# A two-layer decoder on one core: the mixers' turned tiles move from SyncE's queue to GpSimd's, and some turns go to TensorE

## The chip, the core and the metric

The kernel runs on one core of one Trainium2 chip. A core has a matrix engine (TensorE, PE in the profile; its weight loads are PEld), a vector engine (VectorE, DVE), a scalar engine (ScalarE, ACT), a general engine (GpSimd, POOL) and SyncE (SP), which here only issues transfers. Each engine works through its own instructions in order, and they wait for one another by semaphores. Data lies in SBUF (128 partitions), matmuls write to PSUM, and transfers (DMA) move data between SBUF and the device's memory. An engine that issues a transfer puts it in its own queue.

The metric is the time of the device in microseconds for one execution. The kernel before took 2466.73 us (median of 3 runs, 2465.54 to 2467.15).

## The reference

Two layers over 256 tokens of width 2048, batch 1. All inputs are float32.

```python
def hybrid_mixer(h, positions, w_in, sinks, lb, attn_gain, hgrn_gain, w_out):
    proj = h @ w_in                                   # 2048 -> 5632
    q, k, v, hq, hf, hi, hg = jnp.split(proj, SPLIT_POINTS, axis=-1)
    q = rope(q.reshape(B, S, N_Q_HEADS, HEAD_DIM), positions)
    k = rope(k.reshape(B, S, N_KV_HEADS, HEAD_DIM), positions)
...
    attn = rms_norm(sliding_window_attention(q, k, v, sinks), attn_gain)
    f = lbf + (1.0 - lbf) * jax.nn.sigmoid(z)         # z = hf
    log_f = jnp.log(f)
    k_in = (1.0 - lbf) * jax.nn.sigmoid(-z)
    hq_ = jax.nn.silu(hq.astype(jnp.float32))
    o = hgrn2_chunkwise(hq_.reshape(shp), k_in.reshape(shp), hi.reshape(...), log_f.reshape(shp))
    o = rms_norm(o, hgrn_gain.reshape(HGRN_HEADS, HGRN_VDIM)).reshape(B, S, HGRN_WIDTH)
    hgrn = (o * jax.nn.silu(hg.astype(jnp.float32))).astype(h.dtype)
    return jnp.concatenate([attn, hgrn], axis=-1) @ w_out

for i in range(DEPTH):                                # DEPTH = 2
    x = x + rms_norm(hybrid_mixer(rms_norm(x, pre_mix_gain[i]), ...), post_mix_gain[i])
    h = rms_norm(x, pre_ffn_gain[i])
    f = (jax.nn.silu(h @ w_ffn_gate[i]) * (h @ w_ffn_up[i])) @ w_ffn_down[i]
    x = x + rms_norm(f, post_ffn_gain[i])
    gate = jax.nn.sigmoid(rms_norm(x, ple_gain[i]) @ w_ple_gate[i])
    x = x + (p[i] @ w_ple_proj[i]) * gate
```

The attention has 16 query heads of 64 over 4 key heads, a window of 128 tokens and a sink for each head. The recurrence `hgrn2_chunkwise` has 8 heads of 128; its gate is f, its query hq, its value hi.

## The kernel before

**Strips.** Every projection is cut into strips of 512 output columns (`strip`, L249). A strip runs over eight chunks of 256 rows of the weight. `load_w` (L239) loads a chunk (512 KB, issued by SyncE, four buffers `wr`), and `split` (L172) makes a high part `wh` on ScalarE (L174) and a low part `wl` on VectorE (L175), eight buffers each. For each half t of the tokens and each 128 rows come three matmuls of 512 columns (L261, L262, L264) into an accumulator `acc` in PSUM; there are four such accumulators and each strip takes two. Without skew a strip has 96 matmuls. When an accumulator is complete, `done(t, ps)` reads it out.

**Ticks.** After each chunk `tick` (L94) counts one up, moves the running generators by one step, and calls what `later(n, fn)` has put off by n ticks. A tick without other work is 12 matmuls. This sets the order in which work is written down; the order on each engine then follows the times that the program's ordering step reckons with, so that independent instructions of one engine can change places.

**Turned tiles.** A matmul takes its left side with the contracted dimension on the partitions, so results have to be turned before they are used again. There are two ways in the kernel. `split_T` (L184) transposes 128x128 blocks on TensorE into a PSUM bank `ms` (four banks, also used by the attention and the recurrence) and splits from there. `shuffled` (L204) turns 32x32 blocks on VectorE (L208) into a buffer b, stores b to a tile `turn` in device memory (L211), and reads it back with four transfers (L214) into a buffer d, from which ScalarE and VectorE go on. All five transfers are issued by SyncE, between the loads of weights. b, d and most short-lived tiles come from the pool `nat`, which has nine buffers.

**The mixer**, in order of its strips: key and value (`done_kv`, L491), two strips of queries (`done_q(half)`, L501), then for each of two groups of four recurrence heads the gate f (`done_f`, L620), the query (`done_q`, L638), the value i (`done_i`, L780) and the output gate g (`done_g`, L803). Keys and queries are rotated with two products on VectorE (L482) and two additions on GpSimd (L489) before they are turned. `attend` (L512) waits five ticks after the turn, copies the tile (L516) and runs the scores (L541), the transposes of the probabilities (L577) and the values (L592) between the strips' matmuls. After the second half it turns the attention's output (L524), and splits it five ticks later. In the recurrence f is turned and read four ticks later (L628, L629), q 5 - t ticks later (L651); with q's second half the generator `levels` (L731) starts, which multiplies queries and keys level by level (L737, L700 with the copies L709, L765), and `out` (L786) makes the output, with a small power on GpSimd (L155). `done_g` multiplies it by the gate's silu (L806, L808), turns it and splits it four ticks later (L229, L230). Slot D is used in turn by `ao`, `qd`, `qf` and the value `hv`.

The output projection follows (four strips over the turned mixer outputs `mix`; chunks 6 and 7 read the last group's), then the feed-forward part, where `done_up` (L867) turns its tiles by `shuffled` except in one case by `split_T`, and the embedding gate, whose `turn` (L932) turns x for the next layer.

Of the kernel before, what the change touches and what calls it, by code (L numbers as in the profile page):

```python
# [11 lines left out]
AF = mybir.ActivationFunctionType  # L12
# [3 lines left out]
P = 128  # L16
# [30 lines left out]
def decoder(ctx: ExitStack, tc: tile.TileContext, x, p, positions, w_in, attn_sinks,  # L47
# [3 lines left out]
    nc = tc.nc  # L51
# [20 lines left out]
    def later(n, fn):  # L72

        queue.append((clock[0] + n, fn))

    marks = {}
# [126 lines left out]

    def shuffled(src, n=4):  # L204


        b = nat((P, n * P))
        V.transpose(b.rearrange("p (q k j) -> p k q j", q=4, k=n),  # L208
                    src.rearrange("p (k q j) -> p k q j", k=n, q=4))
        m = dp.tile([4, 32, 4, n * 32], F32, tag="turn", name="turn")  # L210
        nc.sync.dma_start(m.rearrange("a i q f -> (a i) (q f)"), b)  # L211
        d = nat((P, n * P))
        for q in range(4):
            nc.sync.dma_start(d[q * 32:(q + 1) * 32].rearrange("i (a f) -> i a f", a=4),  # L214
                              m[:, :, q].rearrange("a i f -> i a f"))
        return d.rearrange("p (a k j) -> p k a j", a=4, k=n)

    def quarters(a):

        return a.rearrange("p k (a j) -> p k a j", a=4)  # L220

    def split_shuffled(d, gcols, hl, t):
        h, lo = (quarters(a[:, :, t * P:(t + 1) * P]) for a in hl)
        if gcols is None:
            split(d, h, lo)
            return
        for b in range(4):
            g = gcols[:, b:b + 1]
            marks["x"] = S.activation(h[:, b], d[:, b], AF.Copy, scale=g)  # L229
            V.scalar_tensor_tensor(lo[:, b], d[:, b], g, h[:, b].bitcast(F32),  # L230
                                   op0=ALU.mult, op1=ALU.subtract)
# [17 lines left out]
    def strip(lhs, w, col, done, nch=8, row0=0, skew=0, psum=None, pre=None):  # L249
# [4 lines left out]
        def part(t, c, lows=(0, 1)):  # L254
            hi, lo = ws[c]
            for k in range(2):
# [6 lines left out]
                if 1 in lows:  # L263
                    marks[t, c] = T.matmul(ps[t], xh, lo[:, k], start=False, stop=last)  # L264

# [189 lines left out]
    for l in range(DEPTH):  # L455
# [35 lines left out]
        def done_kv(t, ps):  # L491
# [6 lines left out]
            d = shuffled(o[:, 0:256], 2)  # L498
            later(8 - t, lambda: S.copy(quarters(kT[:, :, t * P:(t + 1) * P]), d))

# [11 lines left out]
        def attend(half, t, o):  # L512
            d = shuffled(o)
            for _ in range(5):
                yield
            S.copy(quarters(qT[half][:, :, t * P:(t + 1) * P]), d)  # L516
            yield
# [90 lines left out]
        class Rec:  # L608
# [11 lines left out]
            def done_f(s, t, ps):  # L620
                z = nat()
                S.activation(z, ps, AF.Copy, scale=rx(t)[:, 0:1])

                d = shuffled(z)

                def turn():
                    cols = slice(t * P, (t + 1) * P)
                    S.activation(quarters(s.f[:, :, cols]), d, AF.Sigmoid)  # L628
                    S.activation(quarters(s.k[:, :, cols]), d, AF.Sigmoid, scale=-1.0)  # L629
                    for h in range(4):  # L630
# [4 lines left out]
                                        None, op0=ALU.mult)  # L635
                later(4, turn)

            def done_q(s, t, ps):  # L638
# [6 lines left out]

                d = shuffled(sg)

                def turn():
                    raw = s.qd[:, :, t, 0:P]
                    cols = slice(t * P, (t + 1) * P)  # L650
                    S.copy(quarters(raw), d)  # L651

# [5 lines left out]
                    if t == 1:  # L658
                        start(s.levels())
                later(5 - t, turn)  # L660

# [141 lines left out]
            def done_g(s, t, ps):  # L803
# [6 lines left out]
                if c not in mix:  # L810
                    mix[c] = new_ck()
                d = shuffled(o)
                later(4, lambda: split_shuffled(d, gain_cols(112, l, 8)[:, 4 * s.grp:4 * s.grp + 4],
                                                mix[c], t))

# [38 lines left out]
        for gi, glen in enumerate(FF_GROUPS):  # L854
            hid = []
            for j in range(glen):
# [10 lines left out]
                def done_up(t, ps, hl=hl, gate=gate, j=j):  # L867
                    V.scalar_tensor_tensor(gate[t], ps, rx2(t)[:, 0:1], gate[t],  # L868
                                           op0=ALU.mult, op1=ALU.mult)
                    if glen == 2 and j == 1:  # L870
                        later(2, lambda g=gate[t], hl=hl: split_T(blocks4(g), None, hl, t))
                        return
                    d = shuffled(gate[t])
                    later(3, lambda: split_shuffled(d, None, hl, t))
# [98 lines left out]
```

## Time and profile before

| | |
|---|---|
| median of 3 runs | 2466.73 us (2465.54 to 2467.15) |
| the profiled execution | 2461.75 us |
| its span, from the first instruction to the last | 2460.0 us |
| matmuls on TensorE (PE) | 11245 |
| VectorE, ScalarE, GpSimd busy | 61%, 48%, 4% |
| transfers of turned tiles | 90 stores, 360 reads |
| one store of 256 KB, from issue to landing (median) | 2.5 us |
| one read of 64 KB (median) | 3.7 us |

The profile is of one execution. Its times are in microseconds from the start of the span. Rows name the line of the kernel, the engine, the operation, the tile written and the tiles read. The waits say who waited for whom; the releaser named is the one that came last. Durations of matmuls are those of a pipeline: each lasts 0.39 us in the records while the next starts 0.23 us after it, so start times tell the pace.

### The profile page before, as it was taken

How to read it: one execution, taken by the hardware profiler on the slowest of the kernel's cores; microseconds unless marked ns; L12 is line 12 of the kernel's file. 1: busy time of each engine (PE TensorE's matmuls, PEld its weight loads, DVE VectorE, ACT ScalarE, POOL GpSimd, SP SyncE). 2: the span in 40 equal slices, each digit the busy share in tenths (PEclk: the TensorE clock that was granted, in tenths of full speed). 3: DMA queues.
4: the chain of work that ended last, by engine and by line, in shares of the span. 5: the costliest groups of instructions: out<-in, count | busy, mean ns of one | idle time of the engine just before them, and what ended most of it. 6: DMA issues, size and time to landing. Idle time of an engine off the chain costs nothing.

```text
span 2460.0 us, 30961 instructions
## 1 busy us (share of the span) xinstructions
PE 2431.3 (99%) x11245; PEld 2005.3 (82%) x11245; DVE 1491.9 (61%) x1991; ACT 1187.0 (48%) x1684; POOL 98.5 (4%) x213
## 2 busy tenths in 40 slices
PE   9999999999999999999999999999999999999999
PEld 7887887888888888887888878878888888888877
DVE  7678866545555554557667688565455555555674
ACT  6564446444434434446556454464444444444463
POOL 3100001000000000001001000010000000000010
PEclk9999999999999999999999999999999999999999
DMA  8665665767667766764775756656677676677753
GB/s 265 200 194 172 203 192 163 231 190 213 208 211 209 211 211 195 226 218 155 249 224 165 218 181 196 204 176 219 189 211 224 198 209 214 207 211 212 221 169 130
DMA packets 299065, 497.60 MB, mean 202 GB/s; under 512 B 23424, under 2 KB 68896, under 8 KB 298912
## 3 DMA queue, kind: packets, MB, share of 16 engines
q1 hardware_dynamic: 298608, 495.54, 65.9%
q8 instruction: 88, 1.44, 0.2%
q14 instruction: 65, 0.53, 0.1%
q10 hardware_dynamic: 240, 0.07, 0.0%
q0 software_dynamic: 64, 0.02, 0.0%
HBM read 470.38 MB, written 25.17 MB: 201 GB/s over the span
## 4 chain that ended last, share of the span: by engine, by line
PE 91%; DVE 3%; DMA 2%; ACT 2%; issue 1%; POOL 0%; SPq 0%; ACTq 0%; DVEq 0%; POOLq 0%
PE acc L261 29%; PE acc L262 29%; PE acc L264 29%; DMA wr<-in_w_in_dram 1%; DVE wl L175 1%; PE ms L592 1%; DMA nat<-turn 1%; PE ms L700 1%; DMA turn<-nat 1%; ACT wh L174 1%; PE ms L189 0%; ACT junk L170 0%; PE ms L737 0%; PE ms L765 0%; ACT nat L560 0%
## 5 line engine op out<-in xcount | busy, mean ns | idle before, releaser
L175 DVE TENSOR_TENSOR wl<-wr,wh 128x1024 fp32r<-128x1024 f32 x840 | 1025.4, 1224 | 828.8 <-ACT wh L174 821.4
L174 ACT CAST wh<-wr 128x1024 fp32r<-128x1024 f32 x840 | 882.9, 1053 | 1085.0 <-PE acc L262 955.0
L261 PE MATMUL acc<-wh,ck 128*128 128x512 f32 x3328 | 1302.3, 392 | 14.6 <-ACT ck L200 4.6
L262 PE MATMUL acc<-wh,ck 128*128 128x512 f32 x3328 | 1300.0, 391 | 1.3 <-DVE ck L201 1.2
L264 PE MATMUL acc<-wl,ck 128*128 128x512 f32 x3328 | 1298.1, 390 | 0.0
L261 PEld LDWEIGHTS acc<-wh,ck 128*128 128x128 f32 x3328 | 625.8, 188 | 152.4 <-ACT ck L200 8.9
L262 PEld LDWEIGHTS acc<-wh,ck 128*128 128x128 f32 x3328 | 625.8, 188 | 134.0 <-DVE ck L201 4.8
L264 PEld LDWEIGHTS acc<-wl,ck 128*128 128x128 f32 x3328 | 625.9, 188 | 128.9
L200 ACT ACTIVATE ck<-ms,gT 128x128 fp32r<-128x128 f32 x160 | 50.3, 370 | 15.0 <-DVE ck L201 7.2
L160 POOL TENSOR_TENSOR tiny<-ssf 128x1 f32<-128x1 f32 x4 | 2.1, 536 | 1361.5 <-ACT junk L170 1361.2
L201 DVE SCALAR_TENSOR_TENSOR ck<-ms,gT,ck 128x128 fp32r<-128x128 f32 x160 | 48.5, 347 | 13.4 <-ACT ck L200 12.9
L208 DVE STREAM_TRANSPOSE nat<-nat 128x512 f32<-128x512 f32 (+1 forms) x68 | 46.9, 690 | 10.5 <-POOL nat L489 9.4
L892 DVE TENSOR_TENSOR macc<-acc,macc 128x512 f32<-128x512 f32 x48 | 33.0, 688 | 5.0 <-PE acc L264 4.5
L862 ACT ACTIVATE nat<-acc,ry 128x512 f32<-128x512 f32 x44 | 30.2, 687 | 10.7 <-PE acc L264 10.7
L229 ACT ACTIVATE ck<-nat,gT 128x128 fp32r<-128x128 f32 x88 | 28.1, 391 | 13.3 <-DMA nat<-turn 13.2
L170 ACT ACTIVATE junk<-x 128x512 f32<-128x512 f32 x48 | 30.3, 631 | 8.6 <-DVE x L925 4.4
L868 DVE SCALAR_TENSOR_TENSOR nat<-acc,ry,nat 128x512 f32<-128x512 f32 x44 | 32.4, 748 | 0.1
L230 DVE SCALAR_TENSOR_TENSOR ck<-nat,gT,ck 128x128 fp32r<-128x128 f32 x88 | 25.5, 348 | 9.5 <-ACT ck L229 9.5
L175 DVE TENSOR_TENSOR ck<-nat,ck 128x512 fp32r<-128x512 f32 x42 | 28.9, 687 | 0.1
L174 ACT CAST ck<-nat 128x512 fp32r<-128x512 f32 x42 | 26.0, 618 | 3.8 <-DVE nat L181 3.8
L560 ACT ACTIVATE nat<-nat,tiny 128x128 f32<-128x128 f32 x64 | 24.8, 389 | 4.3 <-DVE tiny L557 4.2
L592 PEld LDWEIGHTS ms<-vv,nat 128*128 128x128 f32 x192 | 23.2, 191 | 3.6 <-ACT nat L580 2.7
(192 smaller groups left out, 886.5 us busy)
## 6 DMA issues: line engine op xcount, KB each, us to landing
wr<-in_w_in_dram SPq DMA_DIRECT2D x176, 512.0 KB, 4.5
wr<-in_w_ffn_gate_dram SPq DMA_DIRECT2D x176, 512.0 KB, 3.9
wr<-in_w_ffn_up_dram SPq DMA_DIRECT2D x176, 512.0 KB, 4.5
wr<-in_w_ffn_down_dram SPq DMA_DIRECT2D x176, 512.0 KB, 4.3
wr<-in_w_out_dram SPq DMA_DIRECT2D x64, 512.0 KB, 4.5
wr<-in_w_ple_gate_dram SPq DMA_DIRECT2D x64, 512.0 KB, 4.6
turn<-nat SPq DMA_DIRECT2D x86, 256.0 KB, 2.5
nat<-turn SPq DMA_DIRECT2D x344, 64.0 KB, 3.7
```

Source lines behind the costliest of these rows:

```text
L170: S.activation(j[:, 0:shape[1]], src, AF.Square, accum_out=acc)
L174: a = S.copy(hi, src)
L175: v = V.tensor_tensor(lo, src, hi.bitcast(F32), op=ALU.subtract)
L200: marks["x"] = S.activation(h[:, b], ps[:, b], AF.Copy, scale=g)
L201: V.scalar_tensor_tensor(lo[:, b], ps[:, b], g, h[:, b].bitcast(F32), op0=ALU.mult, op1=ALU.subtract)
L208: V.transpose(b.rearrange("p (q k j) -> p k q j", q=4, k=n), src.rearrange("p (k q j) -> p k q j", k=n, q=4))
L261: T.matmul(ps[t], xh, hi[:, k], start=first, stop=False)
L262: T.matmul(ps[t], xl, hi[:, k], start=False, stop=False)
L264: marks[t, c] = T.matmul(ps[t], xh, lo[:, k], start=False, stop=last)
L592: T.matmul(po[:, j], e[:, j], vv[:, u, kv * 64:(kv + 1) * 64], start=i == 0, stop=i == len(parts) - 1)
L868: V.scalar_tensor_tensor(gate[t], ps, rx2(t)[:, 0:1], gate[t], op0=ALU.mult, op1=ALU.mult)
L892: V.tensor_tensor(m, ps, m, op=ALU.add)
```

## The change

`shuffled` gets an argument that says which engine issues its five transfers. It is GpSimd unless the caller says otherwise; the feed-forward says otherwise and stays on SyncE. The gate f and the query of the recurrence, in both groups, and the mixer output of the second group, are no longer turned by `shuffled` but by four transposes on TensorE each. Several delays change: the query tile of the attention from 5 ticks to 6, f from 4 to 2, the recurrence's query from 5 - t to 3 - t, the output of the first group from 4 to 6, of the second from 4 to 2. The value returned by `shuffled` is put in a list, and a mark is set that nothing reads.

```diff
-    def shuffled(src, n=4):
+    def shuffled(src, n=4, slow=True):
...
-        nc.sync.dma_start(m.rearrange("a i q f -> (a i) (q f)"), b)
+        e = G if slow else nc.sync
+        e.dma_start(m.rearrange("a i q f -> (a i) (q f)"), b)
...
-            nc.sync.dma_start(d[q * 32:(q + 1) * 32].rearrange("i (a f) -> i a f", a=4),
-                              m[:, :, q].rearrange("a i f -> i a f"))
+            e.dma_start(d[q * 32:(q + 1) * 32].rearrange("i (a f) -> i a f", a=4),
+                        m[:, :, q].rearrange("a i f -> i a f"))
...
         def attend(half, t, o):
             d = shuffled(o)
-            for _ in range(5):
+            for _ in range(6):
                 yield
...
             def done_f(s, t, ps):
...
-                d = shuffled(z)
                 def turn():
+                    pt = bank((P, 4, P))
+                    for b in range(4):
+                        T.transpose(pt[:, b], z[:, b * P:(b + 1) * P], ident)
                     cols = slice(t * P, (t + 1) * P)
-                    S.activation(quarters(s.f[:, :, cols]), d, AF.Sigmoid)
-                    S.activation(quarters(s.k[:, :, cols]), d, AF.Sigmoid, scale=-1.0)
+                    S.activation(s.f[:, :, cols], pt, AF.Sigmoid)
+                    S.activation(s.k[:, :, cols], pt, AF.Sigmoid, scale=-1.0)
...
-                later(4, turn)
+                later(2, turn)
...
             def done_q(s, t, ps):
...
-                d = shuffled(sg)
                 def turn():
+                    pt = bank((P, 4, P))
+                    for b in range(4):
+                        T.transpose(pt[:, b], sg[:, b * P:(b + 1) * P], ident)
...
-                    S.copy(quarters(raw), d)
+                    S.copy(raw, pt)
...
-                later(5 - t, turn)
+                later(3 - t, turn)
...
             def done_g(s, t, ps):
...
+                gcols = gain_cols(112, l, 8)[:, 4 * s.grp:4 * s.grp + 4]
+                if s.grp == 1:
+                    later(2, lambda: split_T(blocks4(o), gcols, mix[c], t))
+                    return
                 d = shuffled(o)
-                later(4, lambda: split_shuffled(d, gain_cols(112, l, 8)[:, 4 * s.grp:4 * s.grp + 4],
-                                                mix[c], t))
+                later(6, lambda: split_shuffled(d, gcols, mix[c], t))
...
-                    d = shuffled(gate[t])
+                    d = shuffled(gate[t], slow=False)
```

More of the change, by code (lines that the diff above doesn't have):

```diff
@@ L210, in shuffled @@
         m = dp.tile([4, 32, 4, n * 32], F32, tag="turn", name="turn")
[L211 removed]
+        e = G if slow else nc.sync
+        e.dma_start(m.rearrange("a i q f -> (a i) (q f)"), b)
         d = nat((P, n * P))
         for q in range(4):
[L214 to L216 removed]
+            e.dma_start(d[q * 32:(q + 1) * 32].rearrange("i (a f) -> i a f", a=4),
+                        m[:, :, q].rearrange("a i f -> i a f"))
+        got = [d.rearrange("p (a k j) -> p k a j", a=4, k=n)]
+        return got
     def quarters(a):
@@ L222, in split_shuffled @@
     def split_shuffled(d, gcols, hl, t):
+        d, = d
         h, lo = (quarters(a[:, :, t * P:(t + 1) * P]) for a in hl)
@@ L263, in part @@
                 if 1 in lows:
-                    marks[t, c] = T.matmul(ps[t], xh, lo[:, k], start=False, stop=last)
+                    marks[t, c] = marks["pe"] = T.matmul(ps[t], xh, lo[:, k], start=False,
+                                                           stop=last)
         for i in range(nch + skew):
@@ L498, in done_kv @@
             d = shuffled(o[:, 0:256], 2)
-            later(8 - t, lambda: S.copy(quarters(kT[:, :, t * P:(t + 1) * P]), d))
+            later(8 - t, lambda: S.copy(quarters(kT[:, :, t * P:(t + 1) * P]), d[0]))
         def done_q(half):
@@ L513, in attend @@
             d = shuffled(o)
-            for _ in range(5):
+            for _ in range(6):
                 yield
-            S.copy(quarters(qT[half][:, :, t * P:(t + 1) * P]), d)
+            S.copy(quarters(qT[half][:, :, t * P:(t + 1) * P]), d[0])
             yield
```

## The prediction, made before the changed kernel was run

> **What bounds the kernel now.** I read the page first, then the waits of TensorE, then the windows by stage, then the timelines around the longest waits. From the page (busy time, share of the span, instructions; chain that ended last):
>
> ```profile
> span 2460.0 us, 30961 instructions
> PE 2431.3 (99%) x11245; PEld 2005.3 (82%) x11245; DVE 1491.9 (61%) x1991; ACT 1187.0 (48%) x1684; POOL 98.5 (4%) x213
> PE 91%; DVE 3%; DMA 2%; ACT 2%; issue 1%; POOL 0%; SPq 0%; ACTq 0%; DVEq 0%; POOLq 0%
> ```
>
> TensorE is the bound: it is idle for 2460.0 - 2431.3 = 28.7 us, and whatever it is given to do in addition lengthens the kernel, unless it goes into one of these holes. Where the holes lie is in the windows (stretch, its length, busy time of PE, PEld, DVE, ACT, POOL): mixer of layer 0, the rest of layer 0 in part, mixer of layer 1.
>
> ```profile
> 60.00:340.00 280.00, 272.34 (x1443) 225.68 (x1442) 211.68 (x388) 145.17 (x262) 16.22 (x24) 1.00 0.63 191
> 440.00:1120.00 680.00, 680.00 (x3001) 561.64 (x3000) 363.00 (x342) 294.84 (x311) 2.00 (x4) 1.00 0.70 210
> 1270.00:1560.00 290.00, 285.09 (x1507) 237.95 (x1506) 217.11 (x390) 150.73 (x267) 16.75 (x22) 1.00 0.63 195
> ```
>
> The feed-forward part has no hole at all; the two mixers, which the change edits, have 7.7 and 4.9 us, 12.6 us together. That is the most that any edit in the mixers can win by removing waits. The waits of TensorE after the start (window from 60 us on; who waits for whom, us in total, times, longest) say what they are; two more rows, of ScalarE, say whether weights are late:
>
> ```profile
> PE acc L261 <- DVE nat L806: 4.1, 2, 2.5
> PE acc L261 <- ACT ck L229: 2.4, 2, 1.6
> PE ms L592 <- ACT nat L580: 1.5, 1, 1.5
> PE acc L261 <- DVE nat L641: 1.2, 1, 1.2
> PE ms L577 <- ACT nat L552: 1.0, 1, 1.0
> PE ms L541 <- ACT qT L516: 0.9, 2, 0.6
> PE ms L700 <- DVE qf L689: 0.7, 1, 0.7
> ```
>
> ```profile
> ACT wh L174 <- PE acc L262: 955.0, 638, 7.2
> ACT wh L174 <- DMA wr<-in_w_in_dram: 35.7, 29, 4.1
> ```
>
> No row of that window has TensorE wait for a weight (wh or wl). The casts that make wh wait 955.0 us for TensorE to free a buffer and 35.7 us for the load: the weights run ahead. So SyncE's queue, from which the change takes 250 of the transfers, bounds nothing, and **relieving it is worth 0 us**; it would be worth something only if the lead of eight chunks were used up.
>
> **The change, part by part.** A turned tile is one 32x32 block transpose on VectorE, one store and four reads. There are 90: 22 in each mixer, 6 at the end of layer 0, 40 in the feed-forward. 20 go to TensorE (8 of the gate f, 8 of the query q, 4 of the last mixer output), 30 go to GpSimd's queue, 40 stay.
>
> *Transposes on TensorE.* The kernel has such groups of four already, in the feed-forward; this is one on TensorE's timeline:
>
> ```profile
> 502.21 0.39 PE L264 MATMUL acc<-wl,ck 128*128 128x512 f32 x1
> 502.44 0.60 PE L189 MATMUL ms<-ident,nat 128*128 128x128 f32 x4
> 502.80 0.47 PE L261 MATMUL acc<-wh,ck 128*128 128x512 f32 x1
> ```
>
> Matmuls start every 0.23 us (502.21 to 502.44). The group begins where the next one would have, and that one starts at 502.80: a group costs 502.80 - 502.44 = 0.36 us. 20 groups make **+7.2 us**. If the 0.60 us of the record were paid in full it would be 12.0. I take 7.2, since the start times show it. A transpose also waits for its tile, and everything behind it in TensorE's order waits too: the row of all 24 such transposes shows no idle time before them:
>
> ```profile
> L189 PE MATMUL ms<-ident,nat 128*128 128x128 f32 x24 | 4.0, 276 | 0.0
> L208 DVE STREAM_TRANSPOSE nat<-nat 128x512 f32<-128x512 f32 x64 | 45.1, 705 | 7.7 <-POOL nat L489 6.6 <-ACT nat L622 0.9
> ```
>
> I cost that wait at 0; its upper end is the 1.2 us of the L641 row for the four q tiles of the first head groups, 4.8. VectorE loses 20 block transposes of 0.705 us, 14 us in all; it is 76% busy in the first mixer (211.68 of 280), so this counts only where TensorE waits for it, below. ScalarE and VectorE read the turned tile from PSUM instead of SBUF in the same number of instructions: 0, hidden under ScalarE's idle half.
>
> *The last mixer output.* Its turned tile is what the first output-projection strip waits for: the two waits on ck L229, 1.6 and 0.8 us. With TensorE transposes two ticks after the strip, instead of a store and four reads and four ticks, the tile is there by tick 3, and chunk 6 needs it. **-2.4 us**; next late would be the order of ScalarE, which already is in the row.
>
> *Gate and query two ticks earlier, with fewer buffers.* The two waits on L806 and the one on L641 are waits for an accumulator whose evacuation was late. ScalarE's timeline in layer 0 shows the evacuations of f, q, g and i, and TensorE's the wait:
>
> ```profile
> 135.44 0.68 ACT L622 ACTIVATE nat<-acc,rx 128x512 f32<-128x512 f32 x1
> ...
> 173.53 0.67 ACT L640 ACTIVATE nat<-acc,rx 128x512 f32<-128x512 f32 x1
> ...
> 199.25 0.69 ACT L805 ACTIVATE nat<-acc,rx 128x512 f32<-128x512 f32 x1 [0.53 <-PE acc L264]
> 212.48 1.27 ACT L783 ACTIVATE hv<-acc,rx 128x512 f32<-128x512 f32 x2 [7.84 <-DVE at L709]
> ```
>
> ```profile
> 175.47 0.50 PE L261 MATMUL acc<-wh,ck 128*128 128x512 f32 x1 [1.17 <-DVE nat L641]
> ```
>
> A strip is 96 matmuls, 21.8 us, but q is evacuated 38 us after f, and i after g, though it is computed before it. In the code q needs one of nine nat buffers while the attention's four turned tiles take two each, and i needs the slot D, which the recurrence frees only after the copies of L709. The change frees two buffers for each f and q tile and starts the recurrence two ticks (5.4 us) earlier. That should remove these waits, 5.3 us, if the buffers are what holds q. Bounds: 0 and -5.3 us; **I take -3.5**, two thirds, because the attention's tiles will hold their buffers longer on GpSimd.
>
> *Stores and reads on GpSimd.* The trace has only small transfers from this queue. Its rows, the two of the same transfer from the groups and from the DMA issues, the add that GpSimd already does in front of a turned tile (ns min/median/max), and a pair of these adds; then the chain of the second query tile on SyncE:
>
> ```profile
> L385 POOL DMA_DIRECT2D sink<-in_attn_sinks_dram x1 | 0.8, 782 | 0.0
> sink<-in_attn_sinks_dram POOLq DMA_DIRECT2D x1, 16.0 KB, 5.3
> L489 POOL TENSOR_TENSOR nat<-nat x24: 454/736/1724, 57.3 to 1320.1; 128x256 f32<-128x256 f32 x16, 128x128 f32<-128x128 f32 x8
> 79.08 1.44 POOL L489 TENSOR_TENSOR nat<-nat 128x256 f32<-128x256 f32 x2 [4.96 <-issue]
> ```
>
> ```profile
> 81.53 0.71 DVE nat L208
> 82.25 2.19 DMA turn<-nat
> 84.52 0.33 SPq L214
> 85.84 4.81 DMA nat<-turn
> 92.34 0.51 ACT qT L516
> ```
>
> On SyncE the tile lands 8.4 us after 82.25 (85.84 + 4.81 = 90.65), and TensorE waits for the copy behind it (the row qT L516). SyncE issues a read in 0.33 to 0.42 us; GpSimd took 0.78 for its one comparable transfer. So a tile takes 0.4 (store) and 4 x 0.36 (reads) = 1.8 us longer; if both landings take 5.3 us as sink's did, instead of 2.2 and 4.8, it is 1.8 + 3.1 + 0.5 = 5.4. The reads wait for the store in GpSimd's own order, and behind them wait the adds of the next query tile: one tile holds GpSimd for 0.8 + 2.2 + 3.1 = 6.1 us. The first tile's store would start near 75 us, so the adds at 79.08 start at 81: 2 us more. A second tile is 3.8 to 7.4 us later than before. The change gives it one tick more, 12 matmuls, 2.7 us. What is left over, 1.1 to 4.7 us, falls on TensorE where it already waits, once in each layer; the second half's query tiles have more room. That is 2.2 to 9.4 us for both layers. Less than nothing it can't be, unless the tick exceeds what GpSimd adds, and then by the 0.9 us of that row. The attention's four output tiles queue 24 us of GpSimd time with no tick added; their reader L229 stands ahead of q's evacuation on ScalarE, 0 to 4 us. From -0.9 to +13.4 I take **+4.5 us**: near the low end for both, since 0.78 us is the one issue time that was measured. The key's, the first group's output's and the layer end's tiles have room of a strip: 0, covered by the lead in the code.
>
> By the Trainium skill, DMA: Bandwidth & Descriptors, section "Issuing engines are not separate DMA queues", issuing from another engine only saves the sequencer's time; the trace agrees, as weights were never late, and the term is 0 by either.
>
> **Sum:** 7.2 - 2.4 - 3.5 + 4.5 = **+5.8 us**. The profiled execution took 2461.75 us (2460.0 span and 1.75 around it), 5 us under the median of the three runs shown, 2466.73. On that median: **2472.5 us**. A measurement of this kernel tells 0.2%, 4.9 us, from no change, so the forecast lies just beyond.
>
> **The rivals.** *Not slower: the nat buffers were the whole cause of the mixers' holes.* Place: q's evacuation around 150 to 175 us in each layer. If it comes at its strip's end, the waits on L641 and L806 go whole (5.3), and with attention less hindered those of L592, L577, L541 and L700 as well (4.1). The sum is 7.2 - 2.4 - 5.3 = -0.5 with the first and -4.6 with all, at GpSimd's cost of 0: 2462 to 2466, 2464 in the middle. It decides as soon as more than 4.8 us is won beyond the projection's wait and GpSimd is hidden. For it speaks the 38 us; against it that GpSimd holds two buffers of each of its tiles longer. Even this case can barely be told from no change, since the holes end at 12.6 us.
>
> *GpSimd is slowed by VectorE.* The adds of L489 take 0.74 us in the median and 1.72 at most: 2.3 times. If half of the issues were so stretched, a tile takes 2.5 us longer to issue, and a second tile, behind its first, 5 us more: some 9 us late, 6 on TensorE after the tick in the first half and, by estimate, half of that in the second, in two layers: 18 in place of 4.5. That is 7.2 - 2.4 - 3.5 + 18 = +19: 2486 us. For it: VectorE is 76% busy there. Against: the medians of that add (0.736 us over 24, both shapes) are near its short time, so most are not stretched. The Trainium skill, SBUF — State Buffer, section "SBUF: two separate sides", says that a transfer issued from GpSimd waits for its descriptors while VectorE holds the port pair that both share; it speaks against this change, and no run so far shows it for a transfer.
>
> *The change doesn't do what it says*, in that the moved issues are placed so that turned tiles come when they do now: then only the transposes and the projection's wait count, 7.2 - 2.4 = +4.8, 2471.5 us, inside the forecast.
>
> **How the numbers follow.** Forecast, 2468 to 2477: 0.45 (the last rival in it). Buffers, 2462 to 2467: 0.25. GpSimd slowed, 2478 to 2495: 0.25. Anything else 0.05. The range 2461 to 2487 leaves out the tail of the third case and half of the rest, under 0.2. Faster than 2461.8 needs nearly every hole closed: 0.12 (half of the second case, as the holes could be 2 to 3 us larger than the idle time counts). Slower than 2471.7: 0.26 of the forecast, all of the third case and 0.03 of the rest, 0.54. The same: 0.34.
>
> **What would show it.** The transposes: 80 more PE matmuls of 0.28 us in groups that cost 0.36. The projection: no wait on L229 at the first output strip. The buffers: q evacuated within a few us of its strip's end, and no waits on L806. GpSimd: issue rows near 0.78 us, and a wait on qT L516 of 1 to 5 us in each layer. Wrong would be the forecast if PE's idle time in the two mixers falls below 5 us, or rises above 25.

## The result and the profile after

The changed kernel takes 2487.62 us (median of 4 runs, 2482.03 to 2489.82); the kernel before, on the same chip, 2466.14 us (4 runs, 2462.82 to 2467.15). The ratio is 1.0088, with a 95% interval from 1.0072 to 1.0103: **slower by about 21 us**. The forecast was 2472.5 us, with a range up to 2487. The sign was right, the size more than three times too small.

The profiled execution took 2482.03 us, the shortest of the four. From its page (span; busy time, share of the span and instructions of each engine):

```profile
span 2480.3 us, 30996 instructions
PE 2442.6 (98%) x11325; PEld 2017.7 (81%) x11325; DVE 1481.7 (60%) x1971; ACT 1184.0 (48%) x1684; POOL 185.9 (7%) x363
```

The span is 20.3 us longer than before's 2460.0. TensorE is busy for 11.3 us more (2442.6 against 2431.3) and idle for 9.0 more (37.7 against 28.7). TensorE's waits from 60 us on (who waits for whom, us in total, times, longest):

```profile
PE ms L546 <- ACT qT L521: 6.9, 3, 3.8
PE ms L656 <- DVE nat L648: 6.7, 2, 5.4
PE acc L265 <- ACT ck L200: 3.0, 4, 1.1
PE ms L189 <- DVE x L936: 2.7, 1, 2.7
```

The three kinds of wait that the change was to remove (before's L806, L229 and L641, 7.7 us together) are gone: nothing later in that answer has them. In their place TensorE waits for the attention's query tile (L546 on qT), for the evacuated query of the recurrence (the transposes L656 on nat L648), and for x at the end of layer 0 (L189 on x L936). In before's rows these had 0.9, 0 (another wait, L641, at that place) and 0.6 us. That is 14.8 us of new waits for 7.7 of old.

Who makes them wait is read one step further back, in ScalarE's waits for turned tiles (same window):

```profile
ACT ck L233 <- DMA nat<-turn: 58.6, 17, 8.5
ACT qT L521 <- DMA nat<-turn: 18.6, 5, 7.1
ACT kT L504 <- DMA nat<-turn: 12.6, 4, 6.0
ACT ck L174 <- DMA nat<-turn: 1.6, 2, 1.1
```

Together 91.4 us. Before, the same answer has one row of any size:

```profile
ACT ck L229 <- DMA nat<-turn: 13.2, 8, 4.3
```

With the smaller waits from the groups (0.6, 0.3 and 0.7 us) that is 14.8. So ScalarE waits 77 us longer for 30 moved tiles, 2.6 us for each. How such a wait gets to TensorE shows on ScalarE's timeline in layer 1 (start, length, engine, line, operation; in brackets the idle time before and its releaser), and then on TensorE's:

```profile
1401.20 1.28 ACT L233 ACTIVATE ck<-nat,gT 128x128 fp32r<-128x128 f32 x4 [8.51 <-DMA nat<-turn]
1402.38 2.92 ACT L174 CAST wh<-wr 128x1024 fp32r<-128x1024 f32 x3
1405.82 0.40 ACT L233 ACTIVATE ck<-nat,gT 128x128 fp32r<-128x128 f32 x1 [0.52 <-DMA nat<-turn]
1406.13 1.25 ACT L647 ACTIVATE nat<-acc,rx 128x512 f32<-128x512 f32 x2
```

```profile
1407.75 1.09 PE L656 MATMUL ms<-ident,nat 128*128 128x128 f32 x4 [5.38 <-DVE nat L648]
```

ScalarE stood for 8.51 us before a late tile of the attention's output (L233). Nobody needed that tile soon. But behind it in ScalarE's order stood the evacuation of the recurrence's query (L647), and for that TensorE waited 5.38 us.

The other half of the loss, more *busy* time, has two parts: 80 more transposes, and a slower clock. The windows after two of the long waits (stretch; its length, then busy time and count of PE, PEld, DVE, ACT and POOL; granted clock, DMA share, GB/s):

```profile
1312.90:1316.30 3.40, 0.32 (x4) 0.32 (x6) 2.68 (x8) 0.97 (x2) 0.00 (x0) 1.00 1.05 349
1316.30:1319.70 3.40, 3.40 (x33) 3.18 (x30) 0.34 (x2) 3.39 (x15) 0.00 (x0) 0.50 0.23 84
1405.00:1412.00 7.00, 4.25 (x15) 3.67 (x16) 7.00 (x13) 4.74 (x10) 2.17 (x4) 0.51 1.00 306
```

In the first of these stretches TensorE waits for qT (3.76 us, to 1316.0); in the second it works without a gap, but at a granted clock of 0.50. The trace has four such stretches after the start, 17.1 us together: at 87.5, 1241.2 and 1316.3 (3.4 us each) and at 1405.1 (6.8 us), each begun during or within 0.6 us after one of the four longest waits. Before has none. At half clock about half the work is done (from 1410.3 us on, matmuls of 512 columns start every 0.43 us instead of every 0.23): up to 8.5 us lost, and about 7 if the 2.75 us in which TensorE stood still in the last window are left out.

The sum nearly closes: 14.8 of new waits, some 7 by the clock and 3.8 for transposes (measured below) are 25.6; less the 7.7 of the old waits, 17.9 of the 20.3 us. The other 2.4 us are not accounted for.

### The profile page after: what moved, and what is told of

Same layout as the page of the kernel before. It is cut to its first block, busy times and chain, and to the rows that moved or that the text cites. A ratio compares the mean times of both kernels' runs of the same rounds, so it can differ in the third digit from the quotient of the medians.

```text
span 2480.3 us, 30996 instructions
## 1 busy us (share of the span) xinstructions
PE 2442.6 (98%) x11325; PEld 2017.7 (81%) x11325; DVE 1481.7 (60%) x1971; ACT 1184.0 (48%) x1684; POOL 185.9 (7%) x363
## 5 line engine op out<-in xcount | busy, mean ns | idle before, releaser
L216 POOL DMA_DIRECT2D nat<-turn x120 | 65.7, 554 | 102.6 <-DMA turn<-nat 41.7
L200 ACT ACTIVATE ck<-ms,gT 128x128 fp32r<-128x128 f32 x176 | 55.6, 369 | 24.5 <-DVE ck L201 13.9
L201 DVE SCALAR_TENSOR_TENSOR ck<-ms,gT,ck 128x128 fp32r<-128x128 f32 x176 | 53.6, 345 | 16.0 <-ACT ck L200 15.4
L233 ACT ACTIVATE ck<-nat,gT 128x128 fp32r<-128x128 f32 x72 | 23.2, 392 | 58.6 <-DMA nat<-turn 58.6
L209 DVE STREAM_TRANSPOSE nat<-nat 128x512 f32<-128x512 f32 (+1 forms) x52 | 35.6, 684 | 15.7 <-POOL nat L494 15.7
```

The costliest lines, as they stand in the source:

```text
L200: marks["x"] = S.activation(h[:, b], ps[:, b], AF.Copy, scale=g)
L201: V.scalar_tensor_tensor(lo[:, b], ps[:, b], g, h[:, b].bitcast(F32), op0=ALU.mult, op1=ALU.subtract)
L209: V.transpose(b.rearrange("p (q k j) -> p k q j", q=4, k=n), src.rearrange("p (k q j) -> p k q j", k=n, q=4))
L216: e.dma_start(d[q * 32:(q + 1) * 32].rearrange("i (a f) -> i a f", a=4), m[:, :, q].rearrange("a i f -> i a f"))
```

## The experiments

Two theories at first. **Q**: the tiles that GpSimd issues land late, late tiles stop ScalarE, and what stands behind stops TensorE. **T**: the cost is on TensorE itself, transposes and what waits for them. "The kernel before" ran on the same chip beside each group of runs: 2463.52 us for the first four runs, 2464.71 for the next, 2465.02 for the last.

**All tiles on SyncE.** TensorE's half of the change alone.

```diff
-    def shuffled(src, n=4, slow=True):
+    def shuffled(src, n=4, slow=False):
```

> The changed kernel with every turned tile issued by SyncE again; the transposes on TensorE and the delays stay as changed. Theory Q (the tiles that GpSimd issues land late and stop TensorE, and each stop also halves its clock): the waits on qT, on the query's transposes and at the end of layer 0 shrink to those of before or less, the clock does not drop after the start, and only the transposes (7.2) less the waits that they remove are left: 2465 to 2471 us. Theory T (the transposes on TensorE and what they wait for are the cost): the time stays near the changed kernel's, 2480 to 2488 us.

Measured: 2460.81 us, ratio 0.9991 (0.9982 to 1.0001), still under Q's range. Its page:

```profile
span 2457.3 us, 30935 instructions
PE 2435.1 (99%) x11325; PEld 2012.2 (82%) x11325; DVE 1481.4 (60%) x1971; ACT 1189.3 (48%) x1686; POOL 101.8 (4%) x213
```

TensorE's busy time is 3.8 us above before's, its idle time 22.2, 6.5 below. There is no stretch at half clock. So the transposes and the earlier gate and query give back about what they cost (the interval just includes no difference; the repetition below lies clear of it), and T falls: the changed kernel's 27 us over this one are GpSimd's.

**Only the 30 tiles on GpSimd.** The other half alone, on the kernel before: gate, query and second output still turned through memory by SyncE.

```diff
+        e = G if slow else nc.sync
+        e.dma_start(m.rearrange("a i q f -> (a i) (q f)"), b)
...
-            for _ in range(5):
+            for _ in range(6):
```

> The kernel before with only the other half of the change: GpSimd issues the same 30 tiles (attention's keys, queries and outputs, first group's output, end of layer 0), with the changed delays for them (6 ticks each); gate, query and second group's output are turned by VectorE and SyncE as before. Theory Q: most of the loss is here, 2474 to 2484 us, with waits on qT of 5 to 8 us and clock drops behind them; less than the changed kernel, since no transpose on TensorE waits for the query. Theory T: within 3 us of before, 2464 to 2469 us.

Measured: 2491.73 us, ratio 1.0107 (1.009 to 1.0123), 28 us over the kernel before, more than Q foretold and more than the whole change loses. TensorE's waits:

```profile
PE acc L262 <- DVE nat L642: 9.6, 2, 4.9
PE ms L542 <- ACT qT L517: 8.5, 2, 4.6
PE ms L189 <- DVE x L926: 5.0, 1, 5.0
PE ms L593 <- ACT nat L581: 3.6, 2, 2.5
```

The late evacuation of the recurrence's query (here TensorE waits for its accumulator), the attention's query tile and x cost TensorE time as in the changed kernel, before any transpose is moved, and there are six stretches at half clock, 37.5 us. Together with the first run: -2.7 for the one half and +28 for the other.

**Only the last mixer output on TensorE.**

```diff
+                if s.grp == 1:
+                    gc = gain_cols(112, l, 8)[:, 4:8]
+                    later(2, lambda: split_T(blocks4(o), gc, mix[c], t))
+                    return
                 d = shuffled(o)
```

> The kernel before with one edit: the second group's mixer output is turned by TensorE, two ticks after its strip. By both theories the two waits at the first output strip (2.4 us in the trace of before) go and four groups of transposes cost 4 x 0.36 = 1.4 us: 1 us faster than before, 2463 to 2468 us.

Measured: 2468.15 us, ratio 1.0016 (1.0007 to 1.0026): 4.6 us slower, a miss. The waits on L229 are gone as foretold, but others came:

```profile
PE acc L261 <- ACT ck L200: 4.8, 4, 2.7
...
PE ms L189 <- DVE ho L808: 2.1, 3, 1.0
```

The transposes wait for their tile ho (2.1 us, which the prediction had at 0), the wait on qT has grown from 0.9 to 3.0 us, and among the waits on L200 (before: 3.0, longest 1.2) is one of 2.7, beside which the clock is halved for 6.8 us.

**More ticks for GpSimd's tiles.** If the tiles are only late, later readers should cure it.

```diff
-            for _ in range(6):
+            for _ in range(8):
...
-                for _ in range(5):
+                for _ in range(10):
...
-                    later(3 if s == 3 else 5 - t, turn)
+                    later(3 if s == 3 else 8 - t, turn)
```

> The changed kernel with longer delays for the readers of the tiles that GpSimd issues: query tile 8 ticks instead of 6, attention's output 10 instead of 5, tiles at the end of layer 0 8 - t instead of 5 - t. Theory Q as a matter of delay only: ScalarE no longer stands waiting for a late tile, the waits on qT, on the query's transposes and on x go, and the time comes to that of the kernel with all tiles on SyncE, 2465 to 2472 us. Theory Q as a matter of GpSimd's queue itself (a pair of tiles holds its queue and its other work whatever the delay): 2476 us or more. Theory T: near the changed kernel, 2480 to 2488 us.

Measured: 2484.55 us, ratio 1.0087 (1.0071 to 1.0102), as slow as the changed kernel. ScalarE's wait stays:

```profile
ACT ck L233 <- DMA nat<-turn: 55.7, 18, 7.5
```

The ticks set when a reader is written down; its place in ScalarE's order follows only in part. At the attention's output it did: the first half of the recurrence's query is evacuated at 153.5 us, against 173.5 in the changed kernel, and no wait on L648 is left, but others have come (4.6 us of L546 on nat L554, 3.2 of L745 on qd). At the end of layer 0 the split of the late tile stands ahead of the gate's evacuation, as it does in the changed kernel:

```profile
1238.22 1.28 ACT L233 ACTIVATE ck<-nat,gT 128x128 fp32r<-128x128 f32 x4 [1.67 <-DMA nat<-turn]
1239.41 0.67 ACT L934 ACTIVATE nat<-acc,rp 128x512 f32<-128x512 f32 x1
```

**One kind of tile at a time back on SyncE,** to see whether the loss can be told off by place. Rival **P**: only the number of moved tiles counts.

```diff
-                d = [shuffled(ao[t][:, h]) for h in range(2)]
+                d = [shuffled(ao[t][:, h], slow=False) for h in range(2)]
```

> The changed kernel with the eight tiles of the attention's output back on SyncE; the key, query, first group's output and layer-end tiles stay on GpSimd. Theory Q (a late tile stops ScalarE, and what stands behind it in ScalarE's order stops TensorE; each long stop then costs a stretch at half clock): the waits of the query's transposes L656 on nat L648 (6.7 us, longest 5.4) go, and with them the 6.8 us at half clock near 1405, 3.4 us: about 10 us off the changed kernel, some 2477. Waits on qT L521 and on x L936 stay. Rival P (the part that is late is not what costs; moving tiles to GpSimd loads a shared path, so that only the number of moved tiles counts): 8 of 30 tiles, a quarter of the 27 us between the changed kernel and the one with all tiles on SyncE, about 7 us, and every wait a little smaller instead of one gone.

The layer end, with `slow=False` in the same way at `shuffled(xr[t][s])`:

> The changed kernel with the six tiles of the layer end (x for the next layer) back on SyncE. Theory Q: the wait of L189 on x L936 falls from 2.7 to the 1.4 us that it has with all tiles on SyncE, and the half clock after it, 3.4 us near 1241, goes (1.7 us): about 3 us off, some 2484 to 2485; waits on qT L521 and nat L648 stay. Rival P: 6 of 30 tiles, about 5 us, spread over all waits.

Key and query, with it at `shuffled(o[:, 0:256], 2)` and in `attend`:

> The changed kernel with the attention's eight query and four key tiles back on SyncE. Theory Q: the waits on qT L521 (6.9 us, 3 times) shrink to about 2 and the two stretches at half clock behind them go (3.4 us): about 8 us off, some 2479; the waits on nat L648 and x L936 stay with their stretches at half clock. Rival P: 12 of 30 tiles, about 11 us, spread over all waits.

And all tiles on GpSimd, but with ScalarE's order set at two of the places. `behind` forbids that what is written under it is issued before the marked instruction; `("ge", 3, 0)` marks the layer end's evacuation in the same way, and the one layer-end tile that goes behind it is read after nine ticks:

```diff
+                marks["qe", l] = S.activation(sg, ps, AF.Sigmoid, scale=rx(t)[:, 0:1])
...
+                while ("qe", l) not in marks:
+                    yield
+                with behind(("qe", l)):
                     for h in range(2):
                         split_shuffled(d[h], gain_cols(96, l, 8)[:, 4 * h:4 * h + 4], attn[h], t)
...
+                            with behind(("ge", 3, 0)) if (s, t) == (2, 1) else nullcontext():
                                 split_shuffled(d, g[:, 4 * s:4 * s + 4], xT[s], t)
```

> The changed kernel, every tile still on GpSimd, but ScalarE's order is set: the splits of the attention's output tiles stand behind the evacuation of the recurrence's query (group 0, both halves), and the split of the last of the layer-end tiles (third strip, second half) behind the evacuation of the last strip's first half. The tiles land as late as before. Theory Q: what costs at these two places is not the lateness but what stands behind it, so the waits on nat L648 and x L936 go, with their stretches at half clock (6.7 - 0 + 2.7 - 1.4 + 3.4 + 1.7): some 13 us off the changed kernel, about 2475; the waits on qT L521 stay, since there TensorE needs the late tile itself. Rival L (the lateness itself costs, whoever stands behind: GpSimd's queue or the buffers held back by it): the wait moves to the next user, and the time stays within 4 us of the changed kernel's 2487.

| kept or put on SyncE | us | ratio (interval) | TensorE idle | at half clock |
|---|---|---|---|---|
| nothing (the changed kernel) | 2487.62 | 1.0088 (1.0072 to 1.0103) | 37.7 | 17.1 |
| attention's output | 2480.99 | 1.0068 (1.0053 to 1.0083) | 36.2 | 13.7 |
| layer end | 2492.66 | 1.0105 (1.008 to 1.013) | 45.0 | 34.1 |
| key and query | 2484.11 | 1.0078 (1.0063 to 1.0093) | 35.1 | 27.3 |
| nothing, but order set | 2485.37 | 1.0081 (1.0064 to 1.0097) | 40.6 | 23.9 |
| everything (first experiment) | 2460.81 | 0.9991 (0.9982 to 1.0001) | 22.2 | 0 |

Idle time is span less busy time of the profiled execution; the last column sums the stretches at a granted clock of 0.5 after 60 us. Theory Q in its simple form fails here. The waits that it named went in two places (L648 with the attention's output on SyncE, and with the order set) and shrank in two (x with the layer end on SyncE; qT, from 6.9 to 2.6 us, with key and query), but with the order set the one on x grew, and the times did not follow. With the attention's output on SyncE:

```profile
PE ms L546 <- ACT qT L521: 8.8, 3, 4.5
PE ms L189 <- DVE x L936: 4.5, 1, 4.5
PE ms L633 <- ACT nat L627: 3.0, 1, 3.0
```

No wait on L648, but 1.9, 1.8 and 2.2 us more at the others. With the layer end on SyncE the wait on x shrinks to 2.0, but another grows:

```profile
PE ms L656 <- DVE nat L648: 12.5, 1, 12.5
```

With the order set, ScalarE evacuates the query ahead of the attention's output tiles, and then stops one step later:

```profile
1407.84 1.26 ACT L650 ACTIVATE nat<-acc,rx 128x512 f32<-128x512 f32 x2
1408.99 1.27 ACT L233 ACTIVATE ck<-nat,gT 128x128 fp32r<-128x128 f32 x4
1415.22 0.40 ACT L233 ACTIVATE ck<-nat,gT 128x128 fp32r<-128x128 f32 x1 [4.95 <-DMA nat<-turn]
1415.53 0.56 ACT L662 COPY qd<-ms 128x512 f32<-128x512 f32 x1
```

```profile
PE ms L549 <- ACT qT L521: 10.0, 3, 4.9
PE ms L748 <- DVE qd L666: 6.5, 2, 4.6
PE ms L189 <- DVE x L940: 5.3, 2, 3.0
```

Now the copy of the transposed query (L662) stands behind the late tile, and TensorE waits for it at L748. Rival P does not hold either. It foretold 7, 5 and 11 us for eight, six and twelve tiles back on SyncE, and every wait a little smaller. Eight made the kernel 7 us faster and twelve 3.5; with six the median is 5 us longer, though its four runs reach from 2482 to 2495 us, so that it is not shown to be slower. And single waits grew, as the rows show. The waits move to whoever is next in ScalarE's order; a single place can't be mended while tiles go on being late. That left the question of what makes them late.

**Where a tile loses its time.** Worked out from the issue and landing records of the 30 tiles, means in us:

| | all on SyncE | changed kernel |
|---|---|---|
| VectorE's turn ends, store issued | 0.12 | 1.02 |
| store issued, landed | 2.72 | 3.63 |
| landed, first read issued | 0.22 | 0.49 |
| four reads issued | 1.78 | 2.26 |
| last read issued, all landed | 3.12 | 3.38 |
| sum | 7.96 | 10.78 |

These are means: tile by tile the changed kernel is from 2.0 us earlier to 8.0 us later. Two experiments vary this lateness: one adds it without GpSimd, the other was to take it away with GpSimd.

Stored twice, nothing on GpSimd:

```diff
-        e = G if slow else nc.sync
+        e = nc.sync
         e.dma_start(m.rearrange("a i q f -> (a i) (q f)"), b)
+        if slow:
+            e.dma_start(m.rearrange("a i q f -> (a i) (q f)"), b)
```

> The kernel with all tiles on SyncE (the first experiment), and each of the 30 tiles that the change gives to GpSimd is stored twice, the second store after the first has landed; nothing is on GpSimd. A tile comes about 3 us later (0.35 us of issue and 2.7 us of landing), as much as GpSimd makes it later on average (10.8 us from the turn on VectorE to the last landing, against 8.0). Theory L (these tiles have no slack: ScalarE's order is laid out for the early time, so lateness of any origin is passed on to ScalarE and about a third of it to TensorE): ScalarE's waits for turned tiles rise from 10 to 60 to 100 us, TensorE's idle time from 22 to some 40, stretches at half clock come, and the time is 2475 to 2490, 15 to 30 us over the first experiment. Rival G (what costs is GpSimd's own queue, its descriptors or its adds held up, not the lateness): within 5 us of the first experiment, 2458 to 2466.

Measured: 2489.23 us, ratio 1.0096 (1.0081 to 1.0111), 27 us over the same kernel with one store (2462.19 on this chip). A tile takes 11.54 us. So a loss of this size needs no tile on GpSimd; whether GpSimd's queue adds something of its own in the changed kernel, which is rival G, this run does not show. The way there was not the one foretold: ScalarE waits only some 24 us for turned tiles, not 60 to 100, and TensorE's loss is at one place:

```profile
PE ms L658 <- DVE nat L650: 25.9, 2, 18.1
```

The longer wait, 18.1 us, is in layer 0. There ScalarE stands 5.96 and 5.55 us for two late tiles of the attention's output (L235, at 182.96 and 189.79) just ahead of the query's evacuation at 190.97: the changed kernel's mechanism, without GpSimd. Before them, and ahead of the evacuation at 1418.15 in layer 1, stand also casts that wait for weights (0.3 to 3.0 us each), since SyncE also loads later when it waits for two stores. How much of the 25.9 us each has can't be told from this run.

Stores on SyncE, reads on GpSimd:

```diff
-        e.dma_start(m.rearrange("a i q f -> (a i) (q f)"), b)
+        nc.sync.dma_start(m.rearrange("a i q f -> (a i) (q f)"), b)
```

> The changed kernel with the 30 stores back on SyncE; the 120 reads stay on GpSimd. The store starts and lands about 1.8 us sooner (0.9 of start, 0.9 of landing); the reads still issue at 0.55 us each. Theory L: about 1 us of lateness for each tile is left, a third of the changed kernel's 2.8, so about a third of its loss: some 9 us over the first experiment, 2466 to 2473, with ScalarE's waits for turned tiles at 30 to 45 us. Rival G (the reads on GpSimd are what costs): 2480 to 2490.

Measured: 2493.34 us, ratio 1.0109 (1.0094 to 1.0123), no better than the changed kernel. The forecast failed because the tiles came no sooner: the store now starts 0.03 us after the turn, but takes 3.71 us to land, and a tile 10.68 in all. So the run can't decide between the theories; the time itself lies nearer to rival G's forecast. SyncE's queue shows why. First all tiles on SyncE, from 63 to 100 us, then the changed kernel in the same stretch, then this one:

```profile
65.36 0.34 SPq L213 DMA_DIRECT2D turn<-nat  x1
65.80 2.95 SPq L246 DMA_DIRECT2D wr<-in_w_in_dram  x2
68.87 2.07 SPq L216 DMA_DIRECT2D nat<-turn  x4
74.10 0.34 SPq L213 DMA_DIRECT2D turn<-nat  x1
74.50 0.97 SPq L246 DMA_DIRECT2D wr<-in_w_in_dram  x2
76.48 1.75 SPq L216 DMA_DIRECT2D nat<-turn  x4
```

```profile
63.19 30.17 SPq L246 DMA_DIRECT2D wr<-in_w_in_dram  x10
```

```profile
76.11 0.34 SPq L213 DMA_DIRECT2D turn<-nat  x1
77.22 5.70 SPq L246 DMA_DIRECT2D wr<-in_w_in_dram  x3
84.58 0.34 SPq L213 DMA_DIRECT2D turn<-nat  x1
85.68 4.98 SPq L246 DMA_DIRECT2D wr<-in_w_in_dram  x2
```

When SyncE has to wait for a store to land, it issues at most two loads and then none until the tile's reads are out: little lies in front of the tile on the transfer engines. When another engine does the waiting, SyncE issues loads of 512 KB one after the other, and the store shares with them. In the records a SyncE store lands after 2.13 us with no load in flight at its issue, 2.55 with one and 3.38 with two (first experiment); GpSimd's take 2.57, 3.39 and 4.16. The mean number in flight is 1.07 in the first experiment, 1.33 in the changed kernel and 1.63 here. A load that has just been issued has more ahead of it than one that is nearly there. Counted by the share of its flight that each load still has ahead, there is 0.33 of a load in front of a store in the first experiment, 0.61 in the changed kernel and 0.72 here, and the landings follow this number (correlations of 0.85 to 0.91 over 30 stores each). A line through the first experiment's stores gives 2.0 us and 2.1 more for each load ahead; by it, some 0.6 of the 0.9 us by which the changed kernel's stores land later are loads in front, and 0.3 are left for GpSimd's own path. This is a reading of the records; no run held the loads back while GpSimd stored.

**The second output back through memory, the rest on SyncE,** and the first experiment once more:

```diff
-                if s.grp == 1:
-                    later(2, lambda: split_T(blocks4(o), gcols, mix[c], t))
-                    return
                 d = shuffled(o)
-                later(6, lambda: split_shuffled(d, gcols, mix[c], t))
+                later(4 if s.grp else 6, lambda: split_shuffled(d, gcols, mix[c], t))
```

> The kernel with all tiles on SyncE, and the second group's output turned by VectorE and SyncE again as in the kernel before (four ticks later); gate and query stay on TensorE. The prediction's step (the last mixer output on TensorE is worth 2.4 us, its four transposes cost 1.4): 1.0 us slower than the first experiment. Rival, from the run of that edit alone, which lost 4.6 us: it is 4 to 5 us faster.

> The first experiment again, as the base of the three others on this chip and to settle whether it is faster than the kernel before: 0.9991 of it the first time, 2 to 3 us. If the prediction's terms for TensorE's half hold (7.2 - 2.4 - 3.5 = +1.3 us) it is the same within 0.2%; as first measured it is 2 to 3 us faster.

Measured: 2459.26 us, ratio 0.9977 (0.9967 to 0.9986), and 2462.19 us, ratio 0.9988 (0.9979 to 0.9996). The first is the fastest kernel of the study, 5.8 us under the kernel before. The two intervals overlap, so that it also beats the first experiment is likely and not certain (2.9 us by the medians on this chip, where the prediction's step had 1.0 us slower and the rival 4 to 5 faster); both beat the kernel before. It has 16 groups of transposes, a busy time 2.4 us over before's, and, like the first experiment, no wait for a split mixer output: the waits on L229 go with gate and query alone.

## Why the prediction was wrong

**Transposes, +7.2.** Too much: busy time rose by 3.8 us in the first experiment and 5.3 in its repetition, of which up to 1.7 belong to a stretch of 3.4 us at half clock near 97.6 us. Their waits, costed at 0 with an upper end of 4.8, were 0.7 us (L633 on L627) with all tiles on SyncE, and 6.7 when GpSimd's tiles were in ScalarE's way.

**The last output, -2.4.** Wrong as an effect of that edit. Alone it takes its two waits away and still loses 4.6 us; beside gate and query it isn't needed for its waits to go.

**Gate and query, fewer buffers, -3.5.** The waits on L806 and L641 are gone in every kernel with these edits, but the buffers are not shown to be the reason. The prediction's sign for them was the query evacuated within a few us of its strip's end. In the first experiment that does not happen: its first half is evacuated 42.1 us after the gate's first half (before: 43.6), and some 16 us after the strip's last matmul in layer 0 (before: 21) and 19 in layer 1 (before: 13), counted at 96 matmuls a strip. It stands on ScalarE directly behind the split of the attention's third output tile, as before. What changed is that its second half comes 0.6 us behind the first, where it came 5.2 us later, behind the fourth tile's split. Two ticks or freed buffers: no run separates them. For the last two terms together the prediction had -5.9; idle time fell by 6.5 and 5.1 us in two profiled executions. So TensorE's half, forecast at 7.2 - 2.4 - 3.5 = +1.3, measured -2.7 and -2.8.

**Stores and reads on GpSimd, +4.5: the step that failed.** It measured +28 alone, and 27 as the difference between the changed kernel and the first experiment (24 by the two ratios, which take out the chips). The upper bound of 13.4 was passed too. What was right in it: a tile was put 1.8 to 5.4 us later, and is 2.8; the waits on qT were to grow by 2.2 to 9.4 us, and grew by 6.0. The issue time is not the 0.78 us that was taken from one transfer of another kind, but 0.55 (groups: line, engine, operation, count, busy time, mean ns, idle time before and what ended it):

```profile
L216 POOL DMA_DIRECT2D nat<-turn x120 | 65.7, 554 | 102.6 <-DMA turn<-nat 41.7 <-issue 38.5 <-PE acc L268 7.9
L213 POOL DMA_DIRECT2D turn<-nat x30 | 17.5, 585 | 65.2 <-DVE nat L209 51.1 <-ACT junk L170 12.0 <-DVE tiny L568 2.1
```

```profile
L216 POOL DMA_DIRECT2D nat<-turn x120: 549/549/732, 66.3 to 1471.4; - x120
```

Three things were wrong. *The room.* The key's, the first output's and the layer end's tiles were put at 0, "covered by the lead in the code", and the attention's output at "0 to 4". The lead in ticks is no room: the readers stand in ScalarE's order about where the tiles used to land, and in the mean the 2.8 us by which a tile is later came out as 2.6 us of ScalarE's waiting. The attention's output then cost 6.7 us and the layer end 2.1. *The clock*, about 7 us, wasn't in the sum at all. *What SyncE does when it is relieved* was put at 0 because weights are never late; but by the records above, the weights that it then loads without a pause lie in front of the stores, for some 0.6 us each.

**The rivals.** "GpSimd is slowed by VectorE" gave 2486 us, close to the result, but by luck, since its mechanism isn't seen: the 120 reads take 549 ns to issue in the least and in the median, and 732 at most, with VectorE 73% busy in the first mixer (204.62 of 280 us in the rows below). The Trainium skill, SBUF — State Buffer, section "SBUF: two separate sides", has GpSimd's transfers held up while VectorE runs an operation that takes both of the shared ports; this trace shows no issue held up, and no run shows how many of VectorE's operations here are of that kind. "The buffers were the whole cause" was right that these waits go, though not about the buffers as far as shown, and wrong of GpSimd. What the prediction said would show the forecast wrong did not: TensorE's idle time in the two mixers is 16.8 us, between its 5 and 25,

```profile
60.00:340.00 280.00, 273.45 (x1470) 229.23 (x1470) 204.62 (x378) 143.27 (x261) 52.76 (x86) 0.99 0.56 170
...
1270.00:1560.00 290.00, 279.75 (x1492) 235.41 (x1491) 206.38 (x372) 143.92 (x256) 50.95 (x81) 0.98 0.56 171
```

since time at half clock counts as busy. The column before the DMA share, 0.99 and 0.98 against before's 1.00, was the one to look at.

## What to carry to other kernels

Before a transfer is moved to another queue, ask what the old queue will do in the time it no longer waits: here, as the records read, its waiting kept weight loads out of the way of the tiles. A delay in the program's order is not slack on an in-order engine; count what stands behind the late reader there, and expect the wait to move on when one reader is moved. And price a wait of TensorE of more than some 2.6 us at its own length and half of the 3.4 or 6.8 us at half clock that came with it.

## What the runs showed of the hardware

**TensorE's clock.** The fourteen traces of this study have 31 waits of TensorE of 2.65 us or more after the start. 30 of them have a granted clock of 0.5 beside them or within 1.5 us behind, for 3.4 us or a multiple of it (6.8, 10.2, 13.7 and 17.1 were seen); the one without was 3.47 us long. Of 17 waits from 1.9 to 2.62 us, five have such a stretch, a sixth has one 2.9 us behind, and eleven have none. The Trainium skill, TensorE: Matmul & The Clock Gate, section "HAM oscillation — how this bites in real kernels", warns of idle gaps above about 3.4 us; here waits of 2.65, 2.72 and 2.75 were enough.

**GpSimd's transfers.** A read is issued in 0.55 us and a store in 0.59; on SyncE it is 0.44 to 0.52 (four reads in 1.75 to 2.07) and 0.34, in the rows above. With no load in flight, a 256 KB store lands in 2.57 us (mean of four) against 2.13 (of five). The Trainium skill, DMA: Bandwidth & Descriptors, section "Specifications", gives about 1 us to the first byte on this path and 0.6 on the other; the difference agrees, on so few stores.
